# A hybrid attention, RG-LRU and memory layer on one core: the second LRU chain in other buffers, the heads' norm moved into the mixing, transposed gates, waits by half a tile, and the order of all engines set anew

## The chip, the cores and the metric

The kernel runs on 1 core of one Trainium2 chip. The metric is the device time of one execution in microseconds, the median of several runs. The engines are called as in the profile: PE (TensorE matmul), PEld (its weight loads), DVE (VectorE), ACT (ScalarE), POOL (GpSimd) and SP (SyncE, which issues the DMAs).

## The reference

One layer for a prompt of 1024 rows and a sample of 32 rows, width 1024, in fp32. Each row is RMS-normed and projected once; the columns of the projection feed three branches, whose outputs are gated, put side by side and projected back.

```
proj = rms_norm(x) @ w_in
dq, dk, dv, dg, lx, lg, mq, mg = split_cols(proj, IN_SIZES)
# A: differential attention, 4 heads, values 128 wide, chunk mask
w = softmax(q0 k0) - lam * softmax(q1 k1)
o = rms_norm(w @ v, da_subln_g) * (1 - lambda_init)      # per head
out_a = o * silu(dg)
# B: RG-LRU, 256 channels: causal conv, two sigmoid gates, linear scan
h[t] = a[t] * h[t-1] + b[t];   out_b = h * silu(lg)
# C: cross attention into 256 memory tokens
out_c = softmax(qm mk) @ mv * silu(mg)
y = x + concat([out_a, out_b, out_c]) @ w_out
```

Keys, values, memory keys and values and the LRU's states are outputs too.

## The kernel before

**Matmuls.** Each fp32 product is made of three matmuls of split operands, high and low part: WH with XH (L601), WL with XH (L602), WH with XL (L603). The helper is `mm3` (L600). The prompt is 8 tiles of 128 rows; the 32 sample rows are tile 8, whose high and low parts lie side by side as 64 stationary columns (XS, L618). The eight blocks of 128 of the contraction are numbered k. `unit_nat` (L606) makes one tile by up to 384 columns with rows on the partitions; `unit_T` (L633) makes the transposed result, 128 columns of the projection on the partitions and 352 of the 1056 rows along the free side.

**Weights.** A weight block is loaded (`wraw`), scaled by the norm's gain and split: ACT makes WH (L586), DVE makes WL (L588).

**Stages on PE.** The projections follow one another as ORDER (L37) says: head 0, lx (LRU input), lg (LRU gate), head 1, dg0 (gate of heads 0 and 1), the memory's mk and mq, heads 2 and 3, dg1. Then comes the output projection, `wo` in four blocks of 256 columns, the first two interleaved by tile, the second LAG tiles behind the first. In between, three lanes of attention items fill in: an item is one head and one tile (`attention`, L792). It makes scores (L823, L824), row maxima on DVE (L830, L833), exponentials on ACT (L836), the difference of the two softmaxes on DVE (P, L847), transposes of P (L858), a split into uh and ul (L431, L433), and the product with the values (L876).

**Heads' norm.** At the end of each item DVE sums the two halves of the result (OP, L885), puts a column for the epsilon beside it (L888), ACT squares and sums (jk, L892), POOL takes the power of minus one half (ssq, L442), DVE scales (L896), and SP stores 128 columns to `o_d` in DRAM. There are 36 items.

**Gates of the heads.** `gate` makes dg in rows (one `unit_nat` per tile and half of the columns), ACT takes tanh (L1058), DVE makes the gate (L1059), and SP stores it to `g_d`.

**Mixing.** `mix_T` (L1175) loads LRU and memory results and their gates, transposed, multiplies on POOL (L1188) and splits into k = 4 to 7 of the mixed tile. `mix_diff` (L1199) waits for all four heads of a tile, loads mg from `g_d` and mn from `o_d`, multiplies on POOL (L1212), transposes on PE (L1216), and ACT (XH, L431) and DVE (XL, L433) split the result into k = 0 to 3. The output units wait for both; the norm's gain and the gate's half are scaled into the weights of `wo`. `out_evac` adds the input on DVE (`on`, L1339).

**LRU.** `lru_chain` (L992) runs twice, 128 channels each. DVE makes the convolution XC (L1004), ACT copies it to XCh (L431), POOL makes XCl (L433), PE the gates RG and IG, then come elementwise steps, and DVE scans (H, L1035). H lies in the buffer of XCh and is stored to `bt_d`. The second chain's XCh takes the same buffer.

**What sets the order.** Every engine executes its instructions in the order in which they are written, and a planner (`Sched`, L130) writes it. The steps are generators with priorities (PR, L39). The planner has a price for each instruction, takes the engine that is free first, and of the steps that could start within a window (wPE, wACT, wDVE, wPOOL in TUNE, L41) the one with the lowest priority number. TUNE also holds a factor on the prices of all engines but PE (F), a margin that PE keeps to the results of other engines (M), how priorities grow old (aging), and how many PSUM banks each use may hold (acc, tr, S, O). So a change of any price or step changes the order everywhere.

Of the kernel before, what the change touches and what calls it, by code (L numbers as in the profile page):

```python
# [243 lines left out]
def c_pool(n):  # L244
    return 150.0 + 2.1 * n
# [6 lines left out]
def c_dma(kb):  # L252
    return 2100.0 + kb * 2.9


def emit(tc, A, Y):
# [78 lines left out]
    WCOLS = 4224  # L335
# [39 lines left out]
    def small_consts():  # L375
# [41 lines left out]
        d = yield POOL, c_pool(1), [d], ts(gs, pc("da_subln_g"), 0.5 * (1.0 - LAMBDA_INIT) * P ** 0.5, None, ALU.mult)  # L417
# [69 lines left out]
    def rope(dst, i, n, c, deps):  # L487
        d3 = dst.rearrange("p (c d) -> p c d", c=c)
        g = yield GET, rt_s
        t1 = ev.t([P, c, 16], "rt1")  # L490
        t2 = ev.t([P, c, 16], "rt2")
        cs = bcast(rope_t[:n, i, 0:16], [n, c, 16])
        sn = bcast(rope_t[:n, i, 16:32], [n, c, 16])
        for o, a, b, op, w in ((t1[:n], d3[:, :, 0:16], cs, ALU.mult, 64), (t2[:n], d3[:, :, 0:16], sn, ALU.mult, 64),
                               (d3[:, :, 0:8], t1[:n, :, 0:8], t2[:n, :, 8:16], ALU.subtract, 32),
                               (d3[:, :, 8:16], t1[:n, :, 8:16], t2[:n, :, 0:8], ALU.add, 32)):
            after = deps if op is ALU.mult else [d]
            d = yield POOL, c_pool(w), after + [g], lambda: G_.tensor_tensor(out=o, in0=a, in1=b, op=op)
        rt_s.rel(d)
        return d  # L500

    def stacks(k, q, deps):
# [17 lines left out]
        for o, x, y, w in lo:  # L520
            d = yield DVE, c_dve(w), [h], lambda: V_.tensor_tensor(out=o, in0=x, in1=y.bitcast(F32), op=ALU.subtract)
# [12 lines left out]
    class Chunk:  # L534
        def __init__(self, n, srcs, scale):
# [6 lines left out]
            self.buf, self.ring = [WH, WL], w_ring  # L542

# [54 lines left out]
    XT = [Event() for _ in range(NT + 1)]  # L598
# [7 lines left out]
    def unit_nat(ch, i, c0, n, last, x_ev=None):  # L606

        xd = yield WAIT, (x_ev or XT)[i]
        g, (acc,) = yield GET, acc_s
        for k in range(KT):  # L610
            wd = yield WAIT, ch.ready[k]
            if i < NT:
                ts = slice(i * P, (i + 1) * P)
                d = yield from mm3(acc[:, :n], XH[:, k, ts], XL[:, k, ts], ch.h(k, c0, n), ch.l(k, c0, n),
                                   k == 0, k == KT - 1, n, [g, xd, wd])
            else:
                for j, w in enumerate((ch.h(k, c0, n), ch.l(k, c0, n))):
                    d = yield PE, c_pe(n, 64), [g, xd, wd], lambda: T_.matmul(  # L618
                        acc[:2 * NS, :n], XS[:, k, :], w, start=(k == 0 and j == 0), stop=(k == KT - 1 and j == 1))
# [30 lines left out]
    def norm_T(src, n, dst_h, dst_l, done, extra=None, prio=None):  # L650
# [135 lines left out]
    P_s, u_s, OP_s, m_s, jk_s = (Slots(2), Slots(1)), Slots(2), Slots(3), Slots(4), Slots(2)  # L786
# [5 lines left out]
    def attention(o, i):  # L792
# [19 lines left out]
        ssq = wk.t([P, 1], "ssq", bufs=4)  # L812
# [31 lines left out]
        d = yield DVE, 75.0, [d], lambda: V_.reciprocal(out=cf[:n], in_=sm[:n, 1, 0:1])
# [7 lines left out]
        for b0 in range(0, nb, 4):  # L852
# [30 lines left out]
        gq = yield GET, OP_s  # L883
        OP = wk.t([P, P + 1], "OP", bufs=3)
# [3 lines left out]
        d = yield DVE, 70.0, [d], lambda: V_.tensor_scalar(out=OP[:n, P:], in0=sm[:n, 0, 0:1], scalar1=(P * EPS) ** 0.5,  # L888
                                                           scalar2=None, op0=ALU.mult)
        yield GET, jk_s  # L890
        jk = wk.t([P, P + 1], "jk", bufs=2)
        d = yield ACT, c_act(128, 0, True), [d], lambda: S_.activation(out=jk[:n], in_=OP[:n], func=AF.Square,  # L892
                                                                       accum_out=ssq[:n])
        jk_s.rel(d)
        d = yield from rsqrt(ssq, ssq, n, 1, [d])
        d = yield DVE, c_dve(128, 1, True), [d], lambda: V_.tensor_scalar(out=OP[:n, :P], in0=OP[:n, :P], scalar1=ssq[:n],  # L896
                                                                          scalar2=None, op0=ALU.mult)
        m_s.rel(d)
        d = yield from dma(o_d[i * P:i * P + n, h * P:(h + 1) * P], OP[:n, :P], [d])
# [92 lines left out]
    def lru_chain(ft, dx):  # L992
# [16 lines left out]
        XCh = lru.t([P, L], "XCh", F32R, tag="XCh")  # L1009
# [3 lines left out]
        IG = lru.t([P, L], "IG")  # L1013
        for g, dst, bn in ((0, RG, "lru_b_a"), (1, IG, "lru_b_x")):
            for c0, cn in ((0, 354), (354, 354), (708, 352)):
# [4 lines left out]
                e = yield ACT, c_act(cn, 1), [d], lambda: S_.activation(out=dst[:, cs], in_=acc[:, :cn], func=AF.Sigmoid,  # L1020
# [13 lines left out]
        H = lru.t([P, L], "H", tag="XCh")  # L1034
# [15 lines left out]
    g_ready = [[Event(), Event()] for _ in range(NT + 1)]  # L1050

    def gate_evac(i, hf, acc, d, done):
        n = rows_of(i)
        if i == NT:
            acc, d = yield from fold_s(acc, 256, d)
        g = yield GET, nat_s
        t = ev.t([P, 512], "nat", bufs=4)
        d = yield ACT, c_act(256), [d, g], lambda: S_.activation(out=t[:n, :256], in_=acc[:n, :256], func=AF.Tanh, scale=0.5), ("exp", "sig")  # L1058
        d = yield DVE, c_dve(256), [d], lambda: V_.scalar_tensor_tensor(  # L1059
            out=t[:n, :256], in0=t[:n, :256], scalar=1.0, in1=acc[:n, :256], op0=ALU.add, op1=ALU.mult)  # L1060
        free_acc(i, acc, d)
        d = yield from dma(g_d[i * P:i * P + n, hf * 256:hf * 256 + 256], t[:n, :256], [d], kb=128)
        nat_s.rel(d)
        done.set(d)
# [530 lines left out]
```

## Time and profile before

| | |
|---|---|
| runs | 596.2, 596.6, 597.46 us, median 596.6 |
| profiled execution | 595.88 us, its span 594.1 us, mean granted clock 0.994 |
| PE busy | 562.3 us (95%) |
| DVE busy | 420.2 us (71%) |
| ACT busy | 342.5 us (58%) |
| POOL busy | 266.8 us (45%) |
| DMA | 57.46 MB, mean 97 GB/s |

The span runs from the first to the last instruction; times inside it are counted from its start. A row of a group gives the line, engine, operation, its output and input, count, busy time and mean ns of one, then the idle time of the engine ahead of them and what ended it. A row of the timeline gives start, duration, and in brackets the idle time before and its releaser. A matmul's end is modelled, so its pace is read from the starts of matmuls that follow one another.

### The profile page before, as it was taken

What the parts mean: (1) busy time and instruction counts of PE and PEld (TensorE: products, weight loads), DVE (VectorE), ACT (ScalarE), POOL (GpSimd) and SP (SyncE); (2) the same over time, 40 slices, a digit from 0 to 9 for tenths busy, and PEclk for the clock granted to TensorE, in tenths of its full rate; (3) what the DMA queues carried; (4) which work ended last, traced back from release to release, by engine and by line L of the source; (5) the groups of instructions that cost most, each with busy time, mean ns of one, the idle gap of its engine ahead of it and who ended that gap; (6) DMA issues with size and microseconds to landing.
All of it is one profiled execution on the core that took longest, in us unless ns stands there. A gap on an engine that the chain in (4) does not pass through costs nothing.

```text
span 594.1 us, 11919 instructions
## 1 busy us (share of the span) xinstructions
PE 562.3 (95%) x3968; PEld 537.9 (91%) x3968; DVE 420.2 (71%) x1084; ACT 342.5 (58%) x944; POOL 266.8 (45%) x479
## 2 busy tenths in 40 slices
PE   2998999997999999999998999999999999989997
PEld 2988999996999999889997999899999989879997
DVE  4777898487358979985559787998799989424111
ACT  5855775838448767775558656665577656212000
POOL 2887732223787402244444668675764422110000
PEclk9999999998999999999998999999999999999999
DMA  8511231122032423330013311310058775423442
GB/s 278 183 56 28 68 97 56 45 74 82 21 108 62 134 80 99 109 91 30 26 44 98 105 43 46 101 48 22 28 163 256 218 214 173 128 86 108 103 100 59
DMA packets 73448, 57.46 MB, mean 97 GB/s; under 512 B 8785, under 2 KB 69578, under 8 KB 73386
## 3 DMA queue, kind: packets, MB, share of 16 engines
q1 hardware_dynamic: 73386, 56.70, 32.2%
q8 instruction: 31, 0.51, 0.3%
q14 instruction: 31, 0.25, 0.1%
HBM read 38.83 MB, written 17.83 MB: 95 GB/s over the span
## 4 chain that ended last, share of the span: by engine, by line
PE 63%; DVE 15%; DMA 5%; issue 5%; ACT 5%; POOL 4%; SPq 1%; POOLq 0%; DVEq 0%; ACTq 0%
PE bank L602 15%; PE bank L603 15%; PE bank L601 15%; PE bank L876 5%; PE bank L618 3%; PE bank L858 2%; DVE WL L588 2%; DMA mn<-o_d 2%; DVE P L847 2%; PE bank L824 2%; PE bank L823 2%; DVE XC L1004 2%; DVE mx L830 1%; SPq L309 1%; POOL rs L442 1%
## 5 line engine op out<-in xcount | busy, mean ns | idle before, releaser
L602 PE MATMUL bank<-WL,XH 128*128 128x256 f32 (+1 forms) x640 | 199.2, 311 | 2.4 <-DVE WL L588 2.2
L601 PE MATMUL bank<-WH,XH 128*128 128x256 f32 (+1 forms) x640 | 198.2, 310 | 1.1 <-ACT XH L431 0.7
L603 PE MATMUL bank<-WH,XL 128*128 128x256 f32 (+1 forms) x640 | 197.3, 308 | 0.4 <-DVE XL L433 0.4
L602 PEld LDWEIGHTS bank<-WL,XH 128*128 128x128 f32 x640 | 121.0, 189 | 4.6 <-DVE WL L588 4.1
L601 PEld LDWEIGHTS bank<-WH,XH 128*128 128x128 f32 x640 | 121.2, 189 | 2.4 <-ACT XH L431 0.9
L603 PEld LDWEIGHTS bank<-WH,XL 128*128 128x128 f32 x640 | 121.3, 190 | 1.3 <-DVE XL L433 0.9
L836 ACT ACTIVATE P<-bank,mx 128x512 f32<-128x512 f32 (+4 forms) x104 | 58.0, 563 | 22.6 <-DVE mx L833 15.7
L442 POOL TENSOR_TENSOR rs<-ss,mhalf 128x4 f32<-128x4 f32 (+1 forms) x47 | 50.9, 1082 | 36.4 <-DVE ss L472 32.1
L830 DVE TENSOR_REDUCE mx<-bank 128x1 f32<-128x512 f32 (+4 forms) x104 | 55.2, 530 | 10.3 <-PE bank L824 9.2
L588 DVE SCALAR_TENSOR_TENSOR WL<-wraw,pcol,WH 128x256 fp32r<-128x256 f32 (+1 forms) x96 | 52.7, 554 | 3.6 <-ACT WH L586 3.2
L586 ACT ACTIVATE WH<-wraw,pcol 128x256 fp32r<-128x256 f32 (+1 forms) x96 | 51.1, 540 | 4.6 <-DMA wraw<-in_w_in 1.9
L442 POOL TENSOR_TENSOR ssq<-ssq,mhalf 128x1 f32<-128x1 f32 (+1 forms) x36 | 22.2, 617 | 59.8 <-ACT jk L892 56.0
L1339 DVE TENSOR_TENSOR on<-bank,on 128x256 f32<-128x256 f32 x32 | 13.5, 421 | 50.2 <-PE bank L603 32.1
L601 PE MATMUL bank<-XH,WH 128*128 128x352 f32 x144 | 47.5, 330 | 0.0
L603 PE MATMUL bank<-XH,WL 128*128 128x352 f32 x144 | 47.0, 326 | 0.0
L602 PE MATMUL bank<-XL,WH 128*128 128x352 f32 x144 | 46.9, 326 | 0.0
L876 PE MATMUL bank<-KV,ul 128*128 128x256 f32 x144 | 37.1, 286 | 2.0 <-DVE ul L433 1.7
L876 PE MATMUL bank<-KV,uh 128*128 128x256 f32 x144 | 37.5, 287 | 0.0
L482 POOL TENSOR_TENSOR nat<-nat,bc_in 128x256 f32<-128x256 f32 (+1 forms) x38 | 30.4, 802 | 11.3 <-DVE nat L475 6.7
L431 ACT ACTIVATE uh<-bank 128x512 fp32r<-128x512 f32 (+5 forms) x56 | 24.9, 447 | 17.9 <-PE bank L858 15.3
L823 PE MATMUL bank<-KV,QA 128*128 128x512 f32 (+3 forms) x96 | 32.8, 343 | 0.0
L847 DVE SCALAR_TENSOR_TENSOR P<-P,cf,P 128x128 f32<-128x128 f32 (+8 forms) x36 | 32.2, 896 | 0.4
(255 smaller groups left out, 1374.0 us busy)
## 6 DMA issues: line engine op xcount, KB each, us to landing
wraw<-in_w_in SPq DMA_DIRECT2D x32, 192.0 KB, 2.6
wraw<-in_w_in SPq DMA_DIRECT2D x48, 128.0 KB, 2.2
xt<-in_x_prompt SPq DMA_DIRECT2D x8, 512.0 KB, 4.5
wraw<-in_w_out SPq DMA_DIRECT2D x32, 128.0 KB, 3.0
on<-in_x_prompt SPq DMA_DIRECT2D x32, 128.0 KB, 2.9
out_yp<-on SPq DMA_DIRECT2D x32, 128.0 KB, 2.4
gt_d<-nat SPq DMA_DIRECT2D x12, 176.0 KB, 1.8
out_vp<-nat SPq DMA_DIRECT2D x32, 64.0 KB, 1.7
```

The source lines that it names most:

```text
L442: d = yield POOL, c_pow(k), deps, lambda: G_.tensor_tensor(out=rs[:n], in0=ss[:n], in1=mhalf[:n].to_broadcast([n, k]), op=ALU.pow)
L482: d = yield POOL, c_pool(w), [ds], lambda: G_.tensor_tensor(out=d3, in0=d3, in1=gain, op=ALU.mult)
L586: d = yield ACT, c_act(n, 1, sb=True), [dd, g, dp, du], lambda: S_.activation(out=h, in_=raw[:, :n], func=AF.Copy, scale=scale(k))
L588: d = yield DVE, c_dve(n, 1), [d], lambda: V_.scalar_tensor_tensor(out=l, in0=raw[:, :n], scalar=scale(k), in1=h.bitcast(F32), op0=ALU.mul ...
L601: yield PE, c_pe(n), deps, lambda: T_.matmul(out, ah, bh, start=first, stop=False)
L602: yield PE, c_pe(n), deps, lambda: T_.matmul(out, ah, bl, start=False, stop=False)
L603: d = yield PE, c_pe(n), deps, lambda: T_.matmul(out, al, bh, start=False, stop=last)
L823: yield PE, c_pe(ln), [g, kd], lambda: T_.matmul(S[:n], QA[:, c], K[:, c, ks], start=True, stop=False)
L830: d = yield DVE, c_dve(ln), [d, gm], lambda: V_.tensor_reduce(out=mx[:n, c, s:s + 1], in_=S[:n], axis=AX.X, op=ALU.max, negate=True)
L836: e = yield ACT, c_act(ln, 1, True), [d, gP], lambda: S_.activation(out=Pc[c][:n, k0:k0 + ln], in_=St[s][:n], func=AF.Exp, bias=mx[:n, c, ...
L847: d = yield DVE, c_dve(nk, 1) + 57.0, [d], lambda: V_.scalar_tensor_tensor(out=Pc[0][:n, :nk], in0=Pc[1][:n, :nk], scalar=cf[:n], in1=Pc[0 ...
L876: t = yield PE, c_pe(256, n), [e, gO, vd], lambda: T_.matmul(O[:n].rearrange("p s e -> p (s e)"), u[:m, b - b0, :n], V[:m, b].rearrange("p ...
```

## The change

Six things change.

1. **LRU buffers.** The second chain's XCh lies in the first chain's IG buffer and its IG in the first one's XCh buffer; H stays in the buffer of its own chain's XCh. Now the second IG's sigmoid waits until the first H is stored.
2. **Heads' norm while mixing.** The attention stores OP unscaled, with the epsilon column beside it, in rows of 129; POOL writes that column, once per item. `mix_diff` loads four heads of 129, ACT squares them (msq, L1198 in the new kernel), DVE sums (mss, L1199), POOL takes the power (mrs, 128x4), and DVE multiplies (mn, L1202): 9 times each, for 36 of each before.
3. **Transposed gates.** dg0 and dg1 are made by `unit_T`, 12 groups in all, and stored transposed in `gt_d`. POOL's product of mn and mg goes; after the transposes DVE multiplies out of PSUM by gate and gain (mg, L1208), and the split reads that product in SBUF. The weights of `wo` are scaled by one half throughout.
4. **Half tiles.** The input's tile sets an event after its first four blocks; a unit waits for the second only at its fifth. Output units walk k as 4, 5, 6, 7, 0, 1, 2, 3 and need `mix_diff` only for the last four.
5. **Rope** takes three POOL instructions in place of four.
6. **Order.** PR and TUNE have other values (LAG 2 to 1; M 100 to 200; F 1.04 to 1.07; S 3 to 4, O 2 to 3, tr 2 to 4 banks at most; the windows of ACT, DVE and PE shorter, POOL's longer), DMAs are priced higher, and there are four OP buffers for three and 4480 weight columns for 4224.

```diff
-TUNE = {"LAG": 2, "O": 2, "PENALTY": 1283, "S": 3, ...
+TUNE = {"LAG": 1, "O": 3, "PENALTY": 1283, "S": 4, ...
...
+            for k in ch.ks:
+            if k == ch.ks[4]:
+                xd = yield WAIT, e1[i]
...
+        gq = yield GET, OP_s
+        OP = wk.t([P, P + 1], "OP", bufs=4)
+        yield POOL, c_pool(1), [d, gq], lambda: G_.tensor_scalar(out=OP[:n, P:], in0=sm[:n, 0, 0:1], ...
...
-        d = yield DVE, 70.0, [d], lambda: V_.tensor_scalar(out=OP[:n, P:], in0=sm[:n, 0, 0:1], ...
-        d = yield ACT, c_act(128, 0, True), [d], lambda: S_.activation(out=jk[:n], in_=OP[:n], func=AF.Square,
-                                                                       accum_out=ssq[:n])
-        d = yield from rsqrt(ssq, ssq, n, 1, [d])
-        d = yield DVE, c_dve(128, 1, True), [d], lambda: V_.tensor_scalar(out=OP[:n, :P], in0=OP[:n, :P], scalar1=ssq[:n],
-        d = yield from dma(o_d[i * P:i * P + n, h * P:(h + 1) * P], OP[:n, :P], [d])
+        d = yield from dma(o_d[i * P:i * P + n, h], OP[:n], [d])
...
-        XCh = lru.t([P, L], "XCh", F32R, tag="XCh")
+        th, ti = ("XCh", "IG") if ft == 0 else ("IG", "XCh")
+        XCh = lru.t([P, L], "XCh", F32R, tag=th)
...
-        IG = lru.t([P, L], "IG")
+        IG = lru.t([P, L], "IG", tag=ti)
-                e = yield ACT, c_act(cn, 1), [d], lambda: S_.activation(out=dst[:, cs], ...
+                e = yield ACT, c_act(cn, 1), [d] + rg_free[1:] * g, lambda: S_.activation(out=dst[:, cs], ...
-        H = lru.t([P, L], "H", tag="XCh")
+        H = lru.t([P, L], "H", tag=th)
...
-        d = yield POOL, c_pool(512), [d], lambda: G_.tensor_tensor(out=mn[:n], in0=mn[:n], in1=gt[:n], op=ALU.mult)
+        d = yield from dma(mn[:n], o_d[t0:t0 + n], od + [g], kb=258)
+        gd = yield from dma(gt[:, :, :n], gt_d[:, 4:8, t0:t0 + n], gd + [g], kb=256)
+        d = yield ACT, c_act(516, sb=True), [d, g], lambda: S_.activation(out=msq[:n], in_=mn[:n], func=AF.Square)
+        d = yield DVE, c_dve(516), [d], lambda: V_.tensor_reduce(out=mss[:n], in_=msq[:n], axis=AX.X, op=ALU.add)
+        d = yield from rsqrt(mrs, mss, n, 4, [d])
+        d = yield DVE, c_dve(512), [d], lambda: V_.tensor_tensor(
+            out=mn[:n, :, :P], in0=mn[:n, :, :P], in1=bcast(mrs[:n], [n, 4, P], 2), op=ALU.mult)
...
+        d = yield DVE, c_dve(4 * n, 1), [t, gd], lambda: V_.scalar_tensor_tensor(
+            out=gt[:, :, :n], in0=tr[:, :, :n], scalar=gs, in1=gt[:, :, :n], op0=ALU.mult, op1=ALU.mult)
...
-                acc, d = yield from unit_nat(ch, i, 0, 256, i == NT)
+            yield from unpaced(gates_T(f"dg{ft}", 4 + 2 * ft))
...
+        chunks[f"wo{c}"].ks = [4, 5, 6, 7, 0, 1, 2, 3]
```

Three places of the order follow. The first is PE at the start of the program; `xt` is an input tile that is transposed, WH and XH are the first head's weights and the first tile. Before:

```order
L352 MATMUL bank_69<-ident,rows 128x41
L676 MATMUL bank_70<-ident,xt 128x128 x4
L676 MATMUL bank_71<-ident,xt 128x128 x4
L676 MATMUL bank_72<-ident,xt 128x128 x4
L601 MATMUL bank_73<-WH,XH 128x384
L602 MATMUL bank_73<-WL,XH 128x384
L676 MATMUL bank_74<-ident,xt 128x128 x4
L603 MATMUL bank_73<-WH,XL 128x384
```

And now, with the products one line further down in the file and the transposes six:

```order
L352 MATMUL bank_68<-ident,rows 128x41
L682 MATMUL bank_69<-ident,xt 128x128 x4
L682 MATMUL bank_70<-ident,xt 128x128 x4
L602 MATMUL bank_71<-WH,XH 128x384
L603 MATMUL bank_71<-WL,XH 128x384
L604 MATMUL bank_71<-WH,XL 128x384
L602 MATMUL bank_71<-WH,XH 128x384
L603 MATMUL bank_71<-WL,XH 128x384
L682 MATMUL bank_72<-ident,xt 128x128 x4
```

Five products of the first unit moved ahead of the second tile's transposes.

The second is ACT around the second chain's XCh; `nat` 352 wide is a gate's tanh, P an attention item's exponentials, `sq` the squares of a head's keys or queries. Before:

```order
L836 ACTIVATE P_1569,sm<-bank_69,mx 128x512
L836 ACTIVATE P_1569,sm<-bank_73,mx 128x512
L967 ACTIVATE nat<-bank_70 128x352
L431 ACTIVATE XCh<-XC 128x1060
L967 ACTIVATE nat<-bank_75 128x352
L836 ACTIVATE P_1650,sm<-bank_76,mx 32x160
L586 ACTIVATE WH<-wraw,pcol 128x384
L892 ACTIVATE jk,ssq<-OP 128x129
```

And now:

```order
L966 ACT_TABLE_LOAD
L966 ACTIVATE nat<-bank_74 128x352
L586 ACTIVATE WH<-wraw,pcol 128x256
L467 ACTIVATE sq<-bank_75 128x4x64
L734 ACTIVATE nat<-bank_75 128x128
L431 ACTIVATE XCh<-XC 128x1060
L586 ACTIVATE WH<-wraw,pcol 128x256
L467 ACTIVATE sq<-bank_68 128x4x64
```

The copy moved from between the gate's tanh and the exponentials of two attention items to a place among a head's evacuations.

The third is DVE where the last tiles are mixed; `on` is an output unit's sum, XS the sample's tile. Before:

```order
L885 TENSOR_REDUCE OP<-bank_72 128x128
L888 TENSOR_SCALAR OP<-sm 128x1
L1339 TENSOR_TENSOR on<-bank_76,on 128x256
L896 TENSOR_SCALAR OP<-OP,ssq 32x128
L896 TENSOR_SCALAR OP<-OP,ssq 128x128
L1339 TENSOR_TENSOR on<-bank_74,on 128x256
L433 TENSOR_TENSOR XL<-bank_73,XH 128x4x128
L1339 TENSOR_TENSOR on<-bank_70,on 128x256
L433 TENSOR_TENSOR XS<-bank_69,XS 128x4x32
L433 TENSOR_TENSOR XL<-bank_71,XH 128x4x128
```

And now:

```order
L1199 TENSOR_REDUCE mss<-msq 128x4
L1332 TENSOR_TENSOR on<-bank_74,on 128x256
L1202 TENSOR_TENSOR mn<-mn,mrs 128x4x128
L1199 TENSOR_REDUCE mss<-msq 32x4
L1208 SCALAR_TENSOR_TENSOR mg<-bank_75,gs,mg 128x512
L1202 TENSOR_TENSOR mn<-mn,mrs 32x4x128
L1332 TENSOR_TENSOR on<-bank_73,on 128x256
L433 TENSOR_TENSOR XL<-mg,XH 128x4x128
L1208 SCALAR_TENSOR_TENSOR mg<-bank_69,gs,mg 128x4x32
L433 TENSOR_TENSOR XS<-mg,XS 128x4x32
```

The scale of an attention item (L896) left this place, and a sum, a product and a gate product per tile came into it, between the sums of output units.

More of the change, by code (lines that the diff above doesn't have):

```diff
@@ L252, in c_dma @@
 def c_dma(kb):
-    return 2100.0 + kb * 2.9
+    return 2100.0 + kb * 3.3
 def emit(tc, A, Y):
@@ L489, in rope @@
         g = yield GET, rt_s
[L490 to L498, printed above, removed]
+        t = ev.t([P, c, 2, 16], "rt")
+        x = d3[:, :, 0:16].rearrange("p c (o e) -> p c o e", o=1).to_broadcast([n, c, 2, 16])
+        cs = rope_t[:n, i].rearrange("p (o a e) -> p o a e", o=1, a=2).to_broadcast([n, c, 2, 16])
+        d = yield POOL, c_pool(32 * c), deps + [g], lambda: G_.tensor_tensor(out=t[:n], in0=x, in1=cs, op=ALU.mult)
+        for o, a, b, op in ((0, 0, 8, ALU.subtract), (8, 8, 0, ALU.add)):
+            d = yield POOL, c_pool(8 * c), [d], lambda: G_.tensor_tensor(
+                out=d3[:, :, o:o + 8], in0=t[:n, :, 0, a:a + 8], in1=t[:n, :, 1, b:b + 8], op=op)
         rt_s.rel(d)
@@ L542, in __init__ @@
             self.buf, self.ring = [WH, WL], w_ring
+            self.ks = list(range(KT))
         def h(self, k, c0, n):
@@ L577, in split_all @@
             n, scale = ch.n, ch.scale
-            for k in range(KT):
+            for k in ch.ks:
                 dd = yield WAIT, ch.got[k]
@@ L596, in norm_g @@
         return pc("norm_g", k)
-    XT = [Event() for _ in range(NT + 1)]
+    XT0, XT = [Event() for _ in range(NT + 1)], [Event() for _ in range(NT + 1)]
     def mm3(out, ah, al, bh, bl, first, last, n, deps):
@@ L684, in norm_T_in @@
                                                                          l.bitcast(F32))
+            if first and hf == 0:
+                first.set(e)
         if slots:
@@ L1046, in lru_chain @@
         d = yield from dma(bt_d[:, ft, T:], H[:, ss_], [d], kb=16)
+        rg_free.append(d)
         lru_done[ft].set(d)
[L1050 to L1064, printed above, removed]
     NM = 256
@@ L1192, in mix_T @@
         bt_s.rel(d)
-        mix_part(i, d)
-    bt_s = Slots(2)
+        mixed_T[i].set(d)
+    bt_s, msq_s = Slots(2), Slots(1)
     mix_up = Event()
@@ L1215, in mix_diff @@
         for h in range(4):
-            t = yield PE, c_pe(128), [d, g], lambda: T_.transpose(tr[:, h, :n], mn[:n, h * P:(h + 1) * P], ident[:n, :n])
-        mn_s.rel(t)
+            t = yield PE, c_pe(128), [d, g], lambda: T_.transpose(tr[:, h, :n], mn[:n, h, :P], ident[:n, :n])
+        d = yield DVE, c_dve(4 * n, 1), [t, gd], lambda: V_.scalar_tensor_tensor(
+            out=gt[:, :, :n], in0=tr[:, :, :n], scalar=gs, in1=gt[:, :, :n], op0=ALU.mult, op1=ALU.mult)
+        tr_s.rel(d, bank)
         h, l = mix_dst(i, slice(0, 4))
-        d = yield from split(h, l, tr[:, :, :n], 4 * n, [t, xd])
-        tr_s.rel(d, bank)
-        mix_part(i, d)
+        d = yield from split(h, l, gt[:, :, :n], 4 * n, [d, xd])
+        mn_s.rel(d)
+        mixed_d[i].set(d)
     def mem_probs(i, src, d, which, o_, gi, done):
@@ L1394, in gates_T @@
                     acc, d = yield from unit_T(chunks[nm], ft * P, grp, ft == 1 and grp == 2)
-                    sc.spawn(silu2(r0 + ft, grp, acc, d), PR["silu"])
+                    sc.spawn(silu2(r0 + ft, grp, acc, d), PR["silu" if r0 < 4 else "gate"])
+                    if nm == ORDER[-1] and ft == 1:
+                        for i in ((0, 1), (2, 3, 4), (5, 6, 7, 8))[grp]:
+                            xfree[i].set(d)
                     yield None
@@ L1468, in projections @@
         for n, (c, i) in enumerate(wo):
-            acc, d = yield from unit_nat(chunks[f"wo{c}"], i, 0, 256, c not in [x for x, _ in wo[n + 1:]], mixed)
+            acc, d = yield from unit_nat(chunks[f"wo{c}"], i, 0, 256, c not in [x for x, _ in wo[n + 1:]], (mixed_T, mixed_d))
             sc.spawn(out_evac(i, c, acc, d), PR["out"])
@@ L1489, in wo_scale @@
     def wo_scale(k):
-        return gs if k < 4 else half
+        return half
     def scale_m(k):
```

87 lines of the change are left out of this document (38 added, 49 removed).

## Prediction

> **What bounds the kernel now.** I read the page's busy line first.
>
> ```profile
> PE 562.3 (95%) x3968; PEld 537.9 (91%) x3968; DVE 420.2 (71%) x1084; ACT 342.5 (58%) x944; POOL 266.8 (45%) x479
> ```
>
> PE is the bound: of a span of 594.1 us it is idle for 31.8. A change can win by giving PE less to stream or by closing its idle time; the other engines matter where PE waits for them. The waits of PE say for whom (us in total, times, longest).
>
> ```profile
> PE bank L676 <- DVE xt L668: 5.6, 3, 3.1
> PE bank L858 <- DVE P L847: 4.6, 4, 3.5
> PE bank L1216 <- POOL mn L1212: 3.5, 4, 1.4
> PE bank L602 <- DVE WL L588: 2.2, 4, 1.2
> ```
>
> These four are the start, the attention beside the LRU, the mixing of the last tiles, and weights that are not split in time. The windows show where, and what the granted clock did (us, PE busy, clock, DMA share, GB/s).
>
> ```profile
> 133.60:137.60 4.00, 0.49 (x4) 0.97 0.13 45
> 137.60:141.60 4.00, 3.85 (x16) 0.60 0.49 145
> 318.00:322.00 4.00, 2.17 (x11) 0.96 0.36 114
> 322.00:326.00 4.00, 3.97 (x17) 0.61 0.34 101
> ```
>
> A gap is paid twice. After four us in which PE worked 0.49, the next four were granted at 0.60; after 2.17 of four, 0.61. At full clock 3.85 us of such work takes about 3.85 x 0.60 = 2.3, so the aftermath costs some 1.5 us.
>
> The last region is that of head 3's attention and the mixing. The first row has PE, PEld, DVE, ACT and POOL busy, then clock, DMA share and GB/s; the others are of DVE alone.
>
> ```profile
> 430.00:530.00 100.00, 94.23 (x742) 89.04 (x741) 78.39 (x211) 54.43 (x158) 35.87 (x44) 1.00 0.62 181
> ...
> 430.00:455.00 25.00, 23.47 (x74) 1.00 0.68 191
> 455.00:480.00 25.00, 23.80 (x62) 1.00 0.85 238
> 505.00:530.00 25.00, 8.77 (x24) 1.00 0.36 114
> ...
> 355.00:380.00 25.00, 20.29 (x62) 1.00 0.22 61
> ```
>
> For 50 us DVE is busy 47.27 us, 94.5%, nearly as full as PE; then its work runs out at 505 while PE still waits for the last tiles.
>
> **Gates of the attention heads (PE).** Before, 384 matmuls 256 wide and 32 for the sample rows; now 12 groups x 24 = 288 matmuls 352 wide. Their pitch is read from starts, since busy times overlap: 18 starts apart, in the LRU gates (352 wide) and in the output projection (256 wide).
>
> ```profile
> 126.00 0.32 PE L601 MATMUL bank<-XH,WH 128*128 128x352 f32 x1
> ...
> 128.87 0.32 PE L601 MATMUL bank<-XH,WH 128*128 128x352 f32 x1
> ```
>
> ```profile
> 518.15 0.28 PE L603 MATMUL bank<-WH,XL 128*128 128x256 f32 x1
> ...
> 520.29 0.29 PE L603 MATMUL bank<-WH,XL 128*128 128x256 f32 x1
> ```
>
> That is 2.87/18 = 0.159 us and 2.14/18 = 0.119 us. 416 x 0.119 = 49.5 against 288 x 0.159 = 45.8: 3.7 less at most, as the 32 sample matmuls load half the columns and may cost less. I take **-3.0** (-2 to -3.7). It is pure streaming, on the bound engine, so nothing hides it.
>
> **Second LRU chain.** Its first copy on ACT goes into the buffer from which the first chain's result is being stored.
>
> ```profile
> 129.35 1.30 DVE L1004 SCALAR_TENSOR_TENSOR XC<-XP,pcol,XC 128x1060 f32<-128x1060 f32 x1
> ...
> 132.71 1.09 ACT L431 ACTIVATE XCh<-XC 128x1060 fp32r<-128x1060 f32 x1 [6.04 <-DMA bt_d<-H]
> ...
> 133.71 0.45 ACT L967 ACTIVATE nat<-bank 128x352 f32<-128x352 f32 x1
> ...
> 134.62 2.76 DVE L847 SCALAR_TENSOR_TENSOR P<-P,cf,P 128x1024 f32<-128x1024 f32 x1
> ```
>
> ACT stood 6.04 us for the store; behind it waited a gate's tanh, then DVE's gate product and, in DVE's order behind that, the attention's P, for which PE stood 3.5 (the longest of that line in its waits). With other buffers XCh can start when XC is ready, 129.35 + 1.30 = 130.65, not at 132.71: the swap alone gives 2.06 us, not 6. The new order does more: a gate's tanh and a head's first evacuations stand ahead of XCh, weights and further evacuations behind it, and no P of the attention. What the stall costs is 3.5 in the gap and 1.5 in the slow clock, 5.0 in all; bounds 2 and 5, and I take **-3.5**, since something else of the crowded stretch comes late next. The added wait, IG's sigmoid for the stored H, is met by then: before it come XCh (1.09 us), POOL's XCl and the whole RG gate, and H had landed at 132.71. If it were not, the evacuations behind it on ACT would wait as they do now.
>
> **Start.** Before, PE's first product stood behind tile 1's transposes; now five products stand ahead of them.
>
> ```profile
> 11.00 0.60 ACT L431 ACTIVATE XH<-bank 128x512 fp32r<-128x512 f32 x1
> 11.63 0.69 DVE L433 TENSOR_TENSOR XL<-bank,XH 128x512 fp32r<-128x512 f32 x1 [2.13 <-ACT XH L431]
> 13.04 1.12 PE L676 MATMUL bank<-ident,xt 128*128 128x128 f32 x4 [3.10 <-DVE xt L668]
> 13.81 0.67 PE L601 MATMUL bank<-WH,XH 128*128 128x384 f32 x1
> ```
>
> Half a tile is ready at 11.60, so it can begin up to 13.81 - 11.60 = 2.2 us sooner (the half-tile event allows it); the weights of the later k still set the pace. I take **-1.5** (0 to -2.2).
>
> **Weights at head 2 and small waits.** The window at 318 lost 1.83 us and then 1.5 to the clock, 3.4 in all, over DVE's WL. DVE sheds 72 small instructions over the attention, and the order now keeps more distance. **-2.0** (0 to -3.4): a gain not tied to one removed wait. [...]
>
> **Mixing and head 3.** DVE's norms leave the attention and return per tile; its costs by groups of before.
>
> ```profile
> L472 DVE TENSOR_REDUCE ss<-sq 128x4 f32<-128x260 f32 x42 | 17.2, 411 | 5.7 <-ACT sq L467 5.5
> L433 DVE TENSOR_TENSOR XL<-bank,XH 128x512 fp32r<-128x512 f32 x24 | 16.2, 684 | 8.3 <-ACT XH L431 8.3
> L896 DVE TENSOR_SCALAR OP<-OP,ssq 128x128 f32<-128x128 f32 x32 | 12.7, 398 | 2.7 <-POOL ssq L442 2.7
> L1059 DVE SCALAR_TENSOR_TENSOR nat<-nat,bank 128x256 f32<-128x256 f32 x16 | 6.4, 406 | 0.6 <-ACT nat L1058 0.6
> L968 DVE SCALAR_TENSOR_TENSOR nat<-nat,bank 128x352 f32<-128x352 f32 x12 | 6.1, 511 | 2.6 <-ACT nat L967 2.6
> L433 DVE TENSOR_TENSOR XL<-bt,XH 128x512 fp32r<-128x512 f32 x8 | 5.9, 734 | 0.0
> L888 DVE TENSOR_SCALAR OP<-sm 128x1 f32<-128x1 f32 x32 | 4.5, 140 | 0.1
> ```
>
> Over the run DVE sheds 36 x (0.398 + 0.140) = 19.4 and gains about as much, but not in the same place. Each full tile now adds mss (516 wide: between 0.41 and twice that, 0.7), mn x mrs (as the SBUF product, 0.73), the gate product from PSUM (512 wide, from 0.511 for 352: 0.7), and its split reads SBUF (0.73 for 0.68): 2.2 us, so 8 x 2.2 + 0.9 for the small tile = 18.5. From this, head 3's own nine norms, 9 x 0.54 = 4.8, and dg1's gate products, 9 x 0.41 - 6 x 0.51 = 0.6, go off. DVE in 430 to 530 thus rises by 13 from 78.4 to **91.5 us**, with PE's 94.2 beside it. At the 94.5% that the rows show, it takes 96.8; at 0.90, 101.7; I take 0.938, 97.5, so **-2.5** of the 5.8 that PE idles there. Bounds: -5.8 (PE never waits) and +13 (the 0.81 of the row at 355: 91.5/0.81 = 113).
>
> What helps is the tail, the chain after the last attention product.
>
> ```profile
> 511.95 0.42 DVE L885 TENSOR_REDUCE OP<-bank 128x128 f32<-128x256 f32 x1 [0.43 <-PE bank L876]
> ...
> 524.03 1.26 POOL L1212 TENSOR_TENSOR mn<-mn,mg 128x512 f32<-128x512 f32 x1 [1.96 <-DMA mn<-o_d]
> ...
> 525.35 0.65 PE L1216 MATMUL bank<-ident,mn 128*128 128x128 f32 x4 [1.42 <-POOL mn L1212]
> ```
>
> ```profile
> o_d<-OP SPq DMA_DIRECT2D x32, 64.0 KB, 1.7
> ...
> mn<-o_d SPq DMA_DIRECT2D x8, 256.0 KB, 4.8
> ```
>
> That is 13.4 us to the transposes. Now it is 0.42 + 1.7 + 4.8, a square (0.63 estimated from ACT's 512-wide copies), mss 0.7, POOL's 128x4 power 1.08 and 0.73: 10.1, and some queueing. Then come transposes 0.65, gate product 0.7, ACT 0.6 and split 0.73, 2.7; the half-tile order lets a unit start on k = 4 to 7, 12 x 0.119 = 1.4 us, before that is needed. In the order about 90 products, 10.7 us, stand between the last attention product and these transposes, so the cover just holds; without it about 1 us per late tile returns. The power's price has its row:
>
> ```profile
> L442 POOL TENSOR_TENSOR rs<-ss,mhalf 128x4 f32<-128x4 f32 x42 | 45.4, 1081 | 27.4 <-DVE ss L472 24.2 <-DVE OP L888 2.3 <-DVE cf L844 0.2
> L442 POOL TENSOR_TENSOR ssq<-ssq,mhalf 128x1 f32<-128x1 f32 x32 | 20.1, 627 | 50.3 <-ACT jk L892 50.1
> ```
>
> POOL sheds 32 x 0.63 and nine products like the 1.26 above, and takes 9 x 1.08, the eps columns and one wider rope product for two; at 45% it bounds nothing. ACT's queue loses 36 squares and gains 9 and two table loads: free while it is at 54% in the late region.
>
> The store now has rows of 516 bytes. [...]
>
> **Sum.** -3.0 - 3.5 - 1.5 - 2.0 - 2.5 = -12.5 from the profiled execution's 595.9 (span 594.1, 1.8 around it): **583.4**. The median of the runs is 596.6, 0.7 above it, within their spread of 596.2 to 597.5.
>
> **Rivals.** *DVE becomes the bound (slower).* For: 94.5% busy already, 13 us more in the same place, and in-order queues, so that head 3's softmax waits behind mss for an ACT square or behind a gate product for a load. Against: DVE had 16 us free from 505 to 530, and the work can spread there. It decides once DVE's share falls below about 0.9, where the term turns positive, and makes the kernel slower below 91.5/(100 + 10)= 0.83, where it eats the other 10 us. At 0.81: 595.9 - 10 + 13 = **599**. 0.15.
> *Stalls only move.* The order is new in every stage; if each closed gap opens elsewhere, what stays is streaming and the swap's 2.06: 595.9 - 3.0 - 2.1 = **591**. For: of 31.8 us idle the four waits name 15.9; the rest is in the first load and many small ones that an order can move. 0.20.
> *A new gap of 3.5 us halves the clock* somewhere, as at 133.6: + 5.0, **588**. 0.08. This includes that the swap does not do what it says, because IG's sigmoid then waits for the store.
> The forecast has 0.52, with 577 to 588 as its own range; 0.05 is for no change, all gains given back.
>
> **Numbers.** The bounds together give 595.9 - 3.7 - 5 - 2.2 - 3.4 - 5.8 = 576 below; above, 599 belongs to the rival whose worse half I leave out. So 575 to 598. A measurement can tell 0.2%, 1.2 us, from no change. Faster: 0.52 + 0.20 + 0.08, less 0.02 for their upper tails, 0.78; same 0.06; slower 0.16.
>
> **What would show it.** The gate groups at a 0.16 pitch with 12 x 24 of them; no ACT wait of XCh for the store, and no 0.60 window near the LRU; PE's first product near 12; DVE about 91 us in the stretch from head 3 on, at 0.93 or more, with PE's waits for the mixing's transposes under 2 us in all. The forecast is wrong if DVE's share there is under 0.9 and PE waits for softmax, if PE's idle time stays near 30 us, or if a window of 0.6 stands in another place.

## The result, and the profile after

The changed kernel takes 588.4 us (587.3 to 591.0 in four runs) against 597.0 (596.2 to 598.2): a ratio of 0.984, 95% interval 0.981 to 0.987. It is faster, as forecast, by 8.6 us where 12.5 were forecast. The forecast of 583.4 was 5 us too low. Between the two profiled executions, 595.88 and 587.6 us, the difference is 8.3: PE's busy time fell by 5.0 and its idle time by 3.3.

The busy line of the page, and the largest waits of PE (us in total, times, longest; the first is for the first loaded rows, 5.4 before):

```profile
PE 557.3 (95%) x3840; PEld 535.2 (91%) x3840; DVE 427.1 (73%) x1031; ACT 333.3 (57%) x867; POOL 253.3 (43%) x451
```

```profile
PE bank L352 <- DMA rows<-in_rows: 5.2, 1, 5.2
PE bank L887 <- DVE ul L433: 4.4, 5, 1.7
PE bank L602 <- ACT XH L431: 3.3, 2, 2.5
PE bank L1268 <- POOL mw L1262: 2.5, 2, 1.3
PE bank L682 <- DVE xt L674: 2.3, 1, 2.3
```

The waits for P at the LRU (L858, 4.6 before) and for the mixing's transposes (L1216, 3.5 before) are gone or small (P has 1.2 left, now L869). Behind the first load, the largest is now for ul, a split inside the attention. Of a span of 585.8 PE is idle for 28.5, where it was 31.8 of 594.1.

Where the time went is read from the same stretches of both kernels (us, PE busy, granted clock, DMA share, GB/s). They are the same in time, not quite in work: the products of dg1 begin at 425.70 now and at 432.75 before. Before:

```profile
0.00:50.00 50.00, 38.12 (x224) 1.00 0.48 154
50.00:125.00 75.00, 72.74 (x461) 1.00 0.21 60
125.00:175.00 50.00, 46.15 (x273) 0.97 0.24 78
175.00:300.00 125.00, 123.70 (x939) 1.00 0.26 78
300.00:325.00 25.00, 23.14 (x164) 0.93 0.22 67
425.00:500.00 75.00, 72.51 (x564) 1.00 0.69 196
500.00:580.00 80.00, 76.72 (x644) 1.00 0.37 106
```

And after:

```profile
0.00:50.00 50.00, 39.66 (x231) 1.00 0.51 159
50.00:125.00 75.00, 74.90 (x481) 1.00 0.22 62
125.00:175.00 50.00, 48.88 (x296) 1.00 0.17 54
175.00:300.00 125.00, 121.95 (x885) 1.00 0.29 88
300.00:325.00 25.00, 20.34 (x145) 1.00 0.28 83
425.00:500.00 75.00, 69.74 (x488) 0.98 0.71 201
500.00:580.00 80.00, 79.95 (x672) 1.00 0.40 105
```

PE's idle time falls at the start by 1.5, from 50 to 125 by 2.2, at the LRU by 2.7 (and the slow clock there is gone), and from 500 to 580 by 3.2: the tail of the mixing is covered, 0.05 of 80 us is left. It grows from 175 to 325 by 4.6, from dg0 over the memory to the start of head 2, and from 425 to 500 by 2.8. The rest, 1.0 less, lies outside these stretches. These windows, of which the third overlaps its neighbours, show that the stretch from 425 to 500 also lost clock:

```profile
464.00:468.00 4.00, 1.81 (x13) 1.00 0.91 250
480.00:484.00 4.00, 2.15 (x11) 0.84 0.68 216
482.00:486.00 4.00, 3.57 (x16) 0.59 0.59 174
484.00:488.00 4.00, 3.92 (x26) 0.73 0.97 282
```

The gap at 480, 1.85 us of idle time, was paid twice; the one at 464, 2.19 us, once.

### The profile page after: what moved, and what is told of

Read it like the earlier page. It is cut to its first block, busy times and chain, and to the rows that moved or that the text cites. A ratio compares the mean times of both kernels' runs of the same rounds, so it can differ in the third digit from the quotient of the medians.

```text
span 585.8 us, 11516 instructions
## 1 busy us (share of the span) xinstructions
PE 557.3 (95%) x3840; PEld 535.2 (91%) x3840; DVE 427.1 (73%) x1031; ACT 333.3 (57%) x867; POOL 253.3 (43%) x451
## 4 chain that ended last, share of the span: by engine, by line
PE 75%; DVE 11%; issue 4%; POOL 3%; DMA 3%; ACT 3%; SPq 1%; DVEq 0%; POOLq 0%; ACTq 0%
PE bank L602 18%; PE bank L603 18%; PE bank L604 18%; PE bank L887 5%; PE bank L869 3%; PE bank L831 2%; PE bank L830 2%; PE bank L624 2%; DVE WL L588 2%; DVE mx L837 2%; DMA xt<-in_x_prompt 1%; PE bank L777 1%; DMA out_yp<-on 1%; POOL rs L442 1%; PE bank L1292 1%
## 5 line engine op out<-in xcount | busy, mean ns | idle before, releaser
L602 PE MATMUL bank<-WH,XH 128*128 128x384 f32 (+1 forms) x512 | 162.0, 316 | 3.3 <-ACT XH L431 3.3
L604 PE MATMUL bank<-WH,XL 128*128 128x384 f32 (+1 forms) x512 | 162.2, 317 | 1.2 <-DVE XL L433 1.2
L603 PE MATMUL bank<-WL,XH 128*128 128x384 f32 (+1 forms) x512 | 162.0, 316 | 1.5 <-DVE WL L588 1.5
L602 PEld LDWEIGHTS bank<-WH,XH 128*128 128x128 f32 x512 | 97.6, 191 | 4.4 <-ACT XH L431 4.1
L602 PE MATMUL bank<-XH,WH 128*128 128x352 f32 x240 | 79.0, 329 | 0.0
L604 PE MATMUL bank<-XH,WL 128*128 128x352 f32 x240 | 78.5, 327 | 0.0
L603 PE MATMUL bank<-XL,WH 128*128 128x352 f32 x240 | 77.8, 324 | 0.0
L602 PEld LDWEIGHTS bank<-XH,WH 128*128 128x128 f32 x240 | 45.1, 188 | 0.7 <-issue 0.2
L603 PEld LDWEIGHTS bank<-XL,WH 128*128 128x128 f32 x240 | 45.2, 188 | 0.3
L604 PEld LDWEIGHTS bank<-XH,WL 128*128 128x128 f32 x240 | 45.2, 188 | 0.2
```

The source lines that it names most:

```text
L602: yield PE, c_pe(n), deps, lambda: T_.matmul(out, ah, bh, start=first, stop=False)
L603: yield PE, c_pe(n), deps, lambda: T_.matmul(out, ah, bl, start=False, stop=False)
L604: d = yield PE, c_pe(n), deps, lambda: T_.matmul(out, al, bh, start=False, stop=last)
```

## The experiments

The changed kernel ran once more, beside the first three experiments below: 589.6 us, ratio 0.984 (0.982 to 0.987).

> The changed kernel as it is, once more, to stand on the same chip beside the three below. Every theory: 587 to 591 us.

**The buffers of the second chain.** First in the new order, taken back:

```diff
-        th, ti = ("XCh", "IG") if ft == 0 else ("IG", "XCh")
+        th, ti = "XCh", "IG"
```

> The changed kernel with the same order, but the second LRU chain's buffers as before, so that its XCh waits for the store of the first H. If the buffers carry the gain at the LRU, 2 to 5 us more than the changed kernel, with a long wait of ACT for the store and PE idle behind it. If the order carries it (XCh stands among a head's evacuations now), within 1 us of the changed kernel, whether or not ACT waits.

592.8 us, ratio 0.990 (0.988 to 0.993): 3.2 us more than the changed kernel's second run. The waits of ACT and of PE in this kernel show the store's landing in front of XCh, and PE's wait for XCl behind it:

```profile
ACT XCh L431 <- DMA bt_d<-H: 6.8, 1, 6.8
```

```profile
PE bank L603 <- POOL XCl L433: 2.1, 1, 2.1
```

PE idles 2.7 us from 125 to 175 where the changed kernel's second run idles 1.1, and the clock there is 0.97 for 1.00. So in the new order the buffers carry 3 us. Then in the old order, put in alone (XCh, IG and H get the same tags as in the change, every engine's order stays):

```diff
+        th, ti = ("XCh", "IG") if ft == 0 else ("IG", "XCh")
-        XCh = lru.t([P, L], "XCh", F32R, tag="XCh")
+        XCh = lru.t([P, L], "XCh", F32R, tag=th)
```

> The kernel before with its own order on every engine, and only the second LRU chain's buffers changed, so that its XCh no longer waits for the store. If the wait's own 2.06 us (132.71 against 130.65) and the slow clock behind it carry the gain, 2 to 3.5 us less than before. If the whole stall was that wait, 5 us less. If PE waits there for DVE's product of the two softmaxes whatever ACT does, within 1 us of before.

599.0 us, ratio 1.000 (0.998 to 1.002): nothing, the third of the answers. XCh did move, from 132.71 to 130.98. The timeline shows why the time stayed:

```profile
132.15 2.46 POOL L433 TENSOR_TENSOR XCl<-XC,XCh 128x1060 fp32r<-128x1060 f32 x1 [2.56 <-ACT XCh L431]
```

```profile
132.22 2.42 DVE L845 SCALAR_TENSOR_TENSOR cf<-cf,neglam,sm 128x1 f32<-128x1 f32 x1
...
134.99 1.27 DVE L847 SCALAR_TENSOR_TENSOR P<-P,cf,P 128x1024 f32<-128x1024 f32 x1
```

A DVE product of one column took 2.42 us, as long as POOL's XCl beside it, and P, for which PE waits, stood behind it. In the kernel before, P itself was caught: the row quoted in the prediction has it at 2.76 us, here it takes 1.27. So P ended at 136.26 in place of 137.38, 1.1 us sooner, and the clock took that back:

```profile
134.00:138.00 4.00, 1.85 (x12) 0.95 0.14 48
138.00:142.00 4.00, 3.38 (x13) 0.50 0.54 156
142.00:146.00 4.00, 4.00 (x21) 0.69 0.21 66
```

Here it was lowered over two windows, against 0.60 in one before. To test this cause, the same kernel with XCl made by DVE at the place in the program where POOL made it, in both chains:

```diff
-        dc = yield from split(XCh, XCl, XC, L, [d, d0], POOL)
+        dc = yield ACT, c_act(L), [d, d0], lambda: S_.activation(out=XCh, in_=XC, func=AF.Copy)
+        dc = yield POOL, c_pool(L), [dc], lambda: V_.tensor_tensor(out=XCl, in0=XC, in1=XCh.bitcast(F32), op=ALU.subtract)
```

> The kernel before with the second chain's buffers changed, as in the run that gave nothing, and XCl made by DVE in place of POOL, the rest in its order. If POOL's XCl, which moved ahead with XCh, held up DVE's product that PE waits for (a product of one column took 2.42 us beside it), 3 to 5 us less than before: the gap is under 2 us and the clock stays. If the gap has another cause, within 1 us of before.

594.7 us, ratio 0.994 (0.991 to 0.996): 3.6 us less than before, and the intervals of the two kernels lie apart.

```profile
131.05 1.26 DVE L1013 TENSOR_TENSOR XCl<-XC,XCh 128x1060 fp32r<-128x1060 f32 x1
132.24 0.21 DVE L845 SCALAR_TENSOR_TENSOR cf<-cf,neglam,sm 128x1 f32<-128x1 f32 x1
...
132.80 1.28 DVE L847 SCALAR_TENSOR_TENSOR P<-P,cf,P 128x1024 f32<-128x1024 f32 x1
```

```profile
134.00:138.00 4.00, 2.77 (x17) 1.00 0.50 153
138.00:142.00 4.00, 4.00 (x29) 1.00 0.31 84
```

The product of one column takes 0.21, and the clock stays. From 125 to 175 PE idles 2.0 us in place of 3.9, and the slow window is gone; the first chain helps too, as from 50 to 125 PE idles 1.6 in place of 2.3. So the stall at the LRU before was two hold-ups in a row: the store held XCh, and then XCl on POOL held DVE. The second is shown. What the first is worth by itself is not: with only the store's wait removed the time stayed, and no run has XCl on DVE with the old buffers.

**DVE in the mixing.** Two kernels with the changed kernel's order, one with the mixing's sum and product on 8 columns (so it leaves out the heads' norm), one with the sum three times. The diff shows the first:

```diff
-out=mss[:n], in_=msq[:n], axis=AX.X
+out=mss[:n], in_=msq[:n, :, :8], axis=AX.X
...
-            out=mn[:n, :, :P], in0=mn[:n, :, :P], in1=bcast(mrs[:n], [n, 4, P], 2), op=ALU.mult)
+            out=mn[:n, :, :8], in0=mn[:n, :, :8], in1=bcast(mrs[:n], [n, 4, 8], 2), op=ALU.mult)
```

> The changed kernel with the same order on every engine, but the mixing's sum and product on DVE cut to 8 columns each (the heads' norm is so left out, and its output is not the reference's). That takes about 9 x 1.0 = 9 us from DVE between 440 and 515. If DVE is the bound there (it was busy 24.85 of 25 us from 475 to 500, and PE lost 9.1 us from 450 to 500), 4 to 7 us less than the changed kernel, and the window of lowered clock near 482 is gone. If the order and the loads set the waits there, 0 to 1.5 us less and the window stays.

> The changed kernel with the same order, but the mixing's sum on DVE done three times: 18 x 0.6 = 11 us more on DVE between 440 and 515. If DVE is the bound there, 7 to 12 us more than the changed kernel. If the order and the loads set the waits, 1 to 4 us more, as in the idle time of DVE after 500 there is room.

With less, 589.2 us, 0.984 (0.982 to 0.987): no gain. With more, 598.7 us, 1.000 (0.998 to 1.002): 9.1 us more, where 18 more sums of 0.69 added 12.4 to DVE. PE, PEld, DVE, ACT and POOL busy in the 50 us, then clock, DMA share and GB/s, first of the changed kernel in its second run, then with less, then with more:

```profile
450.00:500.00 50.00, 44.89 (x330) 42.52 (x330) 48.23 (x103) 29.97 (x73) 20.49 (x19) 0.97 0.86 251
```

```profile
450.00:500.00 50.00, 45.29 (x322) 42.28 (x321) 42.84 (x106) 30.68 (x75) 19.03 (x19) 0.97 0.86 250
```

```profile
450.00:500.00 50.00, 40.02 (x259) 36.97 (x257) 48.17 (x92) 26.48 (x63) 18.48 (x16) 0.90 0.79 223
```

DVE fell from 48.2 to 42.8 and PE stayed at 45. My theory that DVE alone holds the stretch fell; what is right of it is the other side: there is little room for more, and part of the price of more is the clock, 0.90 for 0.97. With less, PE's waits near 482 do shrink, from 1.9 us to 0.8, but at 493 a wait of 1.4 for XH opens, behind the load of mn, for which ACT stood 3.5.

**The loads of the mixing.** The loads of the LRU and memory results and of their gates cut to one of four blocks (into two fixed buffers that are filled once), alone and with the short sum and product:

```diff
-        d1 = yield from dma(bt[:, :, :n], bt_d[:, :, t0:t0 + n], ds + [g], kb=256)
-        d2 = yield from dma(gt[:, :, :n], gt_d[:, 0:4, t0:t0 + n], ds + [g], kb=256)
+        d1 = yield from dma(bt[:, 0:1, :n], bt_d[:, 0:1, t0:t0 + n], ds + [g], kb=256)
+        d2 = yield from dma(gt[:, 0:1, :n], gt_d[:, 0:1, t0:t0 + n], ds + [g], kb=256)
```

> The changed kernel with its order, but the mixing's two loads of the LRU and memory results and their gates take a quarter of their columns (three quarters of k = 4 to 7 are so left out, filled with a constant; the output is not the reference's; four small fills on POOL are new). If these loads set the waits from 450 to 500 (POOL's product waited 13.8 us for them, and ACT stands behind it in turn), 3 to 5 us less than the changed kernel. If DVE sets them, 0 to 1 us less.

> The same short loads, and the mixing's sum and product on DVE cut to 8 columns as well. If DVE and the loads hold the stretch together, each as long as the other stands, 5 to 8 us less than the changed kernel, where each alone gave little. If neither does and it is the order in which PE, ACT and DVE meet, 0 to 2 us less.

590.0 us, 0.985 (0.982 to 0.988), and 586.9 us, 0.980 (0.977 to 0.984). The loads alone give nothing. Both together give some 2.5 us: that is just above the second answer, 0 to 2, and far from the 5 to 8 of the first, and the interval overlaps that of the changed kernel's second run. With both:

```profile
450.00:500.00 50.00, 44.72 (x332) 41.48 (x331) 45.76 (x104) 29.25 (x71) 20.53 (x19) 1.00 0.65 185
```

DMA fell from 0.86 to 0.65 and PE is idle for 5.3 us as before; what this kernel gained is the clock, 1.00 for 0.97. So neither these 5 us of DVE's work nor these loads hold PE there. What is left is how the steps of head 3's attention and of the mixing follow one another on in-order queues. The trace of the changed kernel shows this for PE's longest wait, for ul:

```profile
464.86 0.84 DVE L588 SCALAR_TENSOR_TENSOR WL<-wraw,half,WH 128x256 fp32r<-128x256 f32 x1
465.63 0.74 DVE L1208 SCALAR_TENSOR_TENSOR mg<-bank,gs,mg 128x512 f32<-128x512 f32 x1
...
466.36 0.41 DVE L433 TENSOR_TENSOR ul<-bank,uh 128x256 fp32r<-128x256 f32 x1
```

```profile
466.82 0.39 PE L887 MATMUL bank<-KV,ul 128*128 128x256 f32 x1 [1.71 <-DVE ul L433]
```

The product with uh started at 464.72, so ul too could have been made then; a split of weights and a gate product stood ahead of it on DVE. Whether another sequence would win was not run. A rival stands untested beside it: POOL's product of the mixing (bt, L1165), which no run shortens, holds up DVE. From 450 to 500 six DVE instructions beside it took 4.0 us longer together than their like without a neighbour, the WL above 0.84 for 0.47. So not all of DVE's 97% is work.

**Gates that come whole sooner.** Transposed gates free the tiles of XH late: the last of two column halves runs over all rows. So the two halves for the first 352 rows first:

```diff
+            a, b = (3, 2) if nm == ORDER[-1] else (2, 3)
+            for u in range(a):
+                for v in range(b):
+                    ft, grp = (v, u) if nm == ORDER[-1] else (u, v)
```

> The changed kernel, with dg1's six transposed units in another sequence: both halves of the columns for the first 352 rows, then for the next, so that the first tiles' gates are whole and their place in XH free after two units, not four. If the mixing starts too late because transposed gates free the tiles late (first output unit right behind dg1 at 460, PE short of work there), 2 to 4 us less than the changed kernel. If PE waits there for the attention of head 3 itself, within 1 us.

594.7 us, 0.993 (0.990 to 0.996): 5 us worse than the changed kernel. Its last stretches (PE busy, clock), in a profiled execution of 598.7, the slowest of its twelve:

```profile
425.00:500.00 75.00, 69.04 (x444) 0.91 0.67 193
500.00:580.00 80.00, 77.86 (x629) 0.96 0.38 103
```

The planner set a new order behind 425, with the clock lowered in two places and a tail that waits again. The theory that the tiles come free too late gets no support, but is not refuted either, since the order changed with it. With XCl on DVE as well, in the same way as above:

> The kernel above, and the LRU's low part XCl made by DVE (1060 wide, 1.3 us as its other products of that width) in the place where POOL made it. POOL's XCl took 2.47 us, and DVE's next product of two SBUF operands did not end before it. If POOL's product holds up DVE's, about 1 us less than the kernel above, and no DVE product of 2 us is left there. If DVE's long products had another cause, 0 to 1.5 us more than the kernel above, as DVE has 2.6 us more to do.

592.0 us, 0.992 (0.989 to 0.996), not to be told from the kernel without it. At the LRU PE is idle for 0.0 us from 125 to 150 where it was 0.7, and the split of weights that stood beside POOL's XCl takes 0.86 instead of 2.02 us; what the end does differs by more than that.

**The order alone.** The numbers PR and TUNE and the DMA prices of the changed kernel in the kernel before, and the reverse:

```diff
-TUNE = {"LAG": 2, "O": 2, ...
+TUNE = {"LAG": 1, "O": 3, ...
-    return 2100.0 + kb * 2.9
+    return 2100.0 + kb * 3.3
```

> The kernel before with the priorities, limits, windows and prices of DMAs of the changed kernel: all engines' order is new, the work is as before, the LRU's buffers too. If the order is what gains (start, small waits, LRU), 3 to 6 us less than before. If the new order serves only the new work, and each closed gap opens elsewhere, within 2 us of before or slower.

> The changed kernel's work and buffers, with the priorities, limits, windows and DMA prices of the kernel before. With the run of the new order on the old work (2.2% slower than before) this completes the square. If the order has to fit the work, this too is slower than before, by 1% or more. If the new work itself carries the gain, 3 to 9 us less than before.

612.2 us, 1.022 (1.019 to 1.025), and 621.8 us, 1.038 (1.034 to 1.042). The first run met the second of its two answers: it lost 14 us. Old work with the old numbers 1.000, old with new 1.022, new with old 1.038, new with new 0.984: neither part carries the gain, each needs the other. The numbers are not the order itself: from them the planner writes another sequence for other work, so this does not show what the old sequence would cost the new work. The new work with the old numbers has the longest stall at the LRU (POOL, then DVE, then PE's busy time and clock):

```profile
125.83 2.44 POOL L433 TENSOR_TENSOR XCl<-XC,XCh 128x1060 fp32r<-128x1060 f32 x1 [0.85 <-ACT XCh L431]
```

```profile
125.89 2.40 DVE L856 SCALAR_TENSOR_TENSOR cf<-cf,neglam,sm 128x1 f32<-128x1 f32 x1
```

```profile
125.00:150.00 25.00, 13.61 (x71) 0.74 0.28 91
```

11.4 of 25 us are idle there, and the clock is 0.74, where the kernel before idles 3.9 in the 50 us from 125.

## Why the prediction was right in sign and too large in size

- **Gates, -3.0.** No run has them alone. Their pitch is as assumed: in dg1, 18 starts from 442.33 on take 2.86 us, 0.159 each, for 288 matmuls. PE's busy time fell by 5.0, which holds the gates' streaming and one slow window less; the term fits.
- **Second LRU chain, -3.5.** PE lost 2.7 us less from 125 to 175, and the clock there is 1.00: about 4 with the 1.5 of the slow clock, so the size was right. The mechanism was half right. The prediction gave the swap alone 2.06 us; alone it gave nothing. It had read P's 2.76 us as P's own length and not seen that POOL's XCl beside it held DVE. It did say that in the new order no P of the attention stands behind XCh, and so it is: what XCl holds there is a split of weights (2.02 us for 0.47), and PE idles 0.7 us from 125 to 150. That the size fits is in part luck, since the hold was not in the sum. In the new order the swap is worth 3.2 us.
- **Start, -1.5.** Right: 1.5 less idle, with the first product at 12.23 for 13.81, behind the same XH:

```profile
12.23 0.69 PE L602 MATMUL bank<-WH,XH 128*128 128x384 f32 x1 [2.47 <-ACT XH L431]
```

- **Weights at head 2 and small waits, -2.0.** This step failed. The small waits up to 125 fell by 2.2, but from 175 to 325 idle time grew by 4.6, now for POOL's memory softmax (mw, 2.5), for ul and P, and for weights; the lowered clock at 318 went, some 1.5. The sum is about +1. Fewer small DVE instructions and the new order's general distance had stood behind this term, and no removed wait; the square of work and numbers shows how little such a guess is worth.
- **Mixing and head 3, -2.5.** This step failed too. The costs of what was added were right: 0.68 for the sum, 0.68 for the product, 0.74 for the gate and 0.68 for the split, 2.1 net per tile for the 2.2 assumed.

```profile
L1208 DVE SCALAR_TENSOR_TENSOR mg<-bank,gs,mg 128x512 f32<-128x512 f32 x8 | 5.9, 742 | 3.2 <-PE bank L1207 3.2
L433 DVE TENSOR_TENSOR XL<-mg,XH 128x512 fp32r<-128x512 f32 x8 | 5.4, 680 | 0.0
L1199 DVE TENSOR_REDUCE mss<-msq 128x4 f32<-128x516 f32 x8 | 5.4, 678 | 0.0
L1202 DVE TENSOR_TENSOR mn<-mn,mrs 128x512 f32<-128x512 f32 x8 | 5.4, 677 | 0.1
```

  What went was priced too low: head 3's norms took 0.68 each in 430 to 530, some of them beside POOL's products, not the run's mean of 0.398. So DVE came to 83.8 us in 430 to 530 (87.3 in 422 to 522, as the stage begins 7 us sooner), not 91.5. The tail is covered as worked out, 3.2 us. But PE idled 2.8 more from 425 to 500 and lost the clock for 1.5: the term came to about +1. DVE's share of these 100 us was 0.84, with 0.97 from 450 to 500 and 0.53 from 505 to 530: the work did not spread as the term's 0.938 had it. The rival that DVE becomes the bound came true on one side only: 12.4 us more on DVE cost 9.1, and taking 5 away gives nothing, so another limit stands right behind it. What that is stays open.
- **Stalls only move.** In part this rival came true: gaps of 9.7 us closed in four stretches and 7.3 opened in two others.
- **A new gap halves the clock.** This rival came true too, in the profiled execution once: 0.59 from 482 to 486, behind 1.85 us of idle time.
- **The signs.** Of those named for the forecast, the pitch, the wait of XCh, the clock at the LRU, the first product and the transposes came as said, DVE's 91 us did not. Two of those named against it came: PE's idle time is 28.5 us, near 30, and a window of 0.6 stands in another place. DVE's share of 0.84 is under the 0.9 named, though PE waits for ul and XH there. The 588.4 lies 0.4 above the forecast's own 577 to 588, beside the rival of a new gap (588).
- **The longer rows.** The load of mn landed in 3.7 us (4.8 before) and mg in 3.3 (4.6); the store in rows of 516 bytes took 2.0 for 1.7. What of this the rows' length did is not shown, since other transfers moved as well.

## What to carry to other kernels

Removing the wait in front of a stall need not remove the stall: look at what the released engine does to the others when it starts sooner. Where all engines follow a written order, new work and new order are one change; test them apart before crediting either. An engine at 97% whose relief gains nothing is not the bound alone, but work added to it can still cost most of its length (9.1 us for 12.4 here). And look for instructions that take longer than their like: their busy time may be another engine's (here the product of one column, 2.42 us beside POOL's XCl for 0.21).

## What the runs showed of the hardware

In these traces POOL products of two SBUF operands held up DVE products of two SBUF operands until they ended or nearly so. Two splits of weights in the changed kernel, one beside POOL's power and one beside its product:

```profile
475.83 1.46 POOL L442 TENSOR_TENSOR mrs<-mss,mhalf 128x4 f32<-128x4 f32 x1 [0.96 <-DVE mx L840]
...
477.69 1.48 POOL L1165 TENSOR_TENSOR bt<-bt,gt 128x512 f32<-128x512 f32 x1 [0.40 <-ACT Wh L586]
```

```profile
476.74 0.47 DVE L588 SCALAR_TENSOR_TENSOR Wl<-wraw,half,Wh 128x256 fp32r<-128x256 f32 x1
...
478.26 1.18 DVE L588 SCALAR_TENSOR_TENSOR Wl<-wraw,half,Wh 128x256 fp32r<-128x256 f32 x1
```

The same split takes 0.47 beside the power and 1.18 beside the product, ending 0.27 behind the product. The LRU agrees: the DVE product of one column took 2.42 beside POOL's XCl, and 0.21 in the run with XCl on DVE. The power held nothing here, though it too reads two SBUF operands and lasts as long, 1.46 to 1.48. A DVE scaling of one SBUF operand by a column of factors was held as well: in the kernel before, OP at 460.36 took 1.37 beside a product of POOL (bt, 1.30 from 460.35), 0.28 without. A DVE instruction that reads PSUM was not: the mixing's gate product took 736 ns beside such a product (2 of them) and 743 without any neighbour (4). A busy-time line does not show this: the split's 1.18 counts as busy in full.

The granted clock fell after a gap of some 2 us in four us (2.15 of 4 us busy from 480 to 484 in the changed kernel, then 0.73), and after 1.81 of 4 busy (464 to 468) it did not. In narrower windows the slow stretches of the two kernels look alike: before, the clock was 0.50 for 3.41 us from 137.36 and again from 321.68, and in the changed kernel 0.50 for 3.42 us from 482.71, each time with 1.00 in the 3.4 us ahead and behind. In the 3.41 us ahead PE was busy for 0.07, 1.58 and 1.55. So a gap of 2 us was a risk of 1.7 more, half of 3.41 by my estimate, and not a sure price: it came behind the gaps at 318 and 480 and not behind the one at 464.
